# The masked products of the RWKV groups per head, over 64 rows, instead of over 128 rows with zeros

## The chip, the cores and the metric

One core of a Trainium2 chip runs the whole program. The metric is the device time of one execution in microseconds (us). TensorE is called PE in the profile (its weight loads PEld), VectorE DVE, ScalarE ACT, GpSimd POOL and SyncE SP.

## The reference

Two networks run one after the other on 512 positions of width 1024. The second has an RWKV mixer in its first layer; that is where the change lies. For each of 8 heads of width 64, and in both directions, the reference runs a scan over 768 positions (256 of context, 512 of the sequence):

```python
def _rwkv7_scan(S0, r, w, k, v, kk, a):
    def step(S, inp):
        r_t, w_t, k_t, v_t, kk_t, a_t = inp
        sa = jnp.einsum('bhvk,bhk->bhv', S, kk_t)
        S = (S * w_t[:, :, None, :] - sa[..., None] * (kk_t * a_t)[:, :, None, :]
             + v_t[..., None] * k_t[:, :, None, :])
        return S, jnp.einsum('bhvk,bhk->bhv', S, r_t)
    xs = tuple(jnp.swapaxes(t, 0, 1) for t in (r, w, k, v, kk, a))
    S, ys = lax.scan(step, S0, xs)
    return jnp.swapaxes(ys, 0, 1), S
```

Everything else of the reference (two blocks of the first network with attention and a convolution, the second network's differential attention, its second layer with two other scans, the MLPs) is computed before or after this stage and is not touched.

## The kernel before

The kernel computes the scan in chunks of 64 positions. Features lie on the partitions: two heads of 64 features fill the 128 rows, so 8 heads are 4 pairs. Each pair has 3 groups of 256 positions (4 chunks) and 2 directions, which makes 4 x 3 x 2 = 24 groups. `rwkv_group` (line 1537) prepares one group without the running state, `rwkv_chain` (line 1667) then carries the state through its 4 chunks.

A group first scales the features by powers of the decay: `AR` (lines 1553 to 1557) holds the scaled kk (index 0) and r (index 1) of each chunk, for each head e in columns of its own. Its tile is [128, 4 chunks, 2 kinds, 2 heads, 64], and the rows of head e are filled only in the columns of head e; the other half was set to zero once, at line 1359, and stays zero. `BK` (lines 1558 to 1560) holds the scaled k·a and k, [128, 4, 2, 64]. Then come the masked products (lines 1563 to 1571): for each chunk j one float32 matmul with BK of the chunk as weights (128 rows, 128 columns) and AR of the chunk as the moving operand (128 rows, 256 columns). Because of the zeros each column gets the sum over one head's 64 rows alone. Two chunks fill a PSUM bank of 512 columns; then DVE multiplies the bank by the causal mask into `Mh`, [128, 4, 2, 2, 64]. A group has 4 such matmuls and 2 such products. Each float32 matmul appears in the trace as two records.

After that ACT copies the part of Mh that belongs to kk to `AV`, one head at a time (line 1581), and a triangular system is solved in five levels: PE lines 1612, 1615 and 1628 (tile `lv`), ACT's copies at 1620 and 1625, DVE's predicated copies at 1602 and 1604, and at the end lines 1633 to 1649. BK and v are transposed at lines 1654 and 1661. In the chain, PE lines 1535, 1682, 1697, 1701 and 1704 (tile `z`) alternate with ACT's copies at 1685, 1693 and 1710 and DVE's update of the state at 1716.

The groups and chains are generators; `rwkv_drive` (line 1364) steps them by turns, up to three groups at once, and beside them the preparation of the next pair (`rwkv_prep`, with PE lines 1443, 1295, 1310) and the end of the last one (`rwkv_post`). The order of the instructions on an engine isn't written out: the framework's planner orders them when the program is built, by its own estimate of when each is ready. The four matmuls of a group stand together in the source, but in the program other lines' work is often put between them. PSUM banks of tag `mm`, three of them, are shared by the masked products, the transposes and the preparation; the levels have three (`lv`) and the chain two (`z`).

Of the kernel before, what the change touches and what calls it, by code (L numbers as in the profile page):

```python
# [15 lines left out]
ALU = mybir.AluOpType  # L16
# [4 lines left out]
P = 128  # L21
# [6 lines left out]
class Build:  # L28
# [1508 lines left out]
    def rwkv_group(self, d, g, n, r, k, v, kk, ka, L):  # L1537

        nc = self.nc
        TT = nc.vector.tensor_tensor  # L1540
# [12 lines left out]
        AR = self.ar[n % RWN[0]]  # L1553
        for e in range(2):
            rows = slice(64 * e, 64 * e + 64)
            TT(out=AR[rows, :, 0, e, :], in0=V4(kk)[rows], in1=G[rows, :, prev], op=ALU.mult)
            TT(out=AR[rows, :, 1, e, :], in0=V4(r)[rows], in1=G[rows, :, now], op=ALU.mult)
        BK = self.tl([P, 4, 2, 64], F32, "bk", "BK")
# [3 lines left out]

        Mh = self.tl([P, 4, 2, 2, 64], F32, "mh", "Mh")
        mk = self.masks[:, MSK[f"mh{d}"][0]:][:, :256]
        for j2 in range(2):
            ps = self.psum("mm")
            for j in (2 * j2, 2 * j2 + 1):
                nc.tensor.matmul(ps[:, (j % 2) * 256:(j % 2) * 256 + 256], BK[:, j].rearrange("p a t -> p (a t)"),  # L1568
                                 AR[:, j].rearrange("p a e t -> p (a e t)"), start=True, stop=True)
            TT(out=Mh[:, 2 * j2:2 * j2 + 2].rearrange("p j a e t -> p j (a e t)"),  # L1570
               in0=ps.rearrange("p (x t) -> p x t", x=2), in1=mk.unsqueeze(1).to_broadcast([P, 2, 256]), op=ALU.mult)
        yield


# [5 lines left out]
        for e in range(2):  # L1580
# [3 lines left out]
            in1=AV[:, :, 32 * d:32 * d + 32], op0=ALU.mult, op1=ALU.add)  # L1584
# [24 lines left out]
        for lev in range(1, 6):  # L1609
            w = 1 << lev  # L1610
            ps = self.psum("lv")
            nc.tensor.transpose(ps[:, 384:512], TV.rearrange("p j t -> p (j t)"), self.ident)
            W = NV if lev < 5 else AV[:, :, 32 * (1 - d):32 * (2 - d)]
            for j in range(4):
                nc.tensor.matmul(ps[32 * j:32 * j + 32, 0:64], W[:, j, :], half(D[:, j, :], d, w),  # L1615
                                 start=True, stop=True, skip_group_check=True)
# [6 lines left out]
            for j in range(4):  # L1623
                rows = slice(32 * j, 32 * j + 32)
# [11 lines left out]
           in1=jm.unsqueeze(1).to_broadcast([P, 2, 4, 32]), op=ALU.mult)  # L1636
# [3 lines left out]
        for b in range(4):  # L1640
            rows = slice(32 * b, 32 * b + 32)
            nc.scalar.copy(out=Tt[rows, :, rows], in_=blocks(F[rows]))
        yield
        for e in range(2):
            rows = slice(64 * e + 32 * d, 64 * e + 32 * d + 32)
            nc.tensor.matmul(ps[rows, 128:256], Bs[:, 32 * e:32 * e + 32], B[:, e].rearrange("p j c -> p (j c)"),
                             start=True, stop=True, skip_group_check=True)
# [4 lines left out]
        ps = self.psum("mm")  # L1652
# [6 lines left out]
        ps = self.psum("mm")  # L1659
# [862 lines left out]
```

## Time and profile before

| | us |
|---|---|
| median of 3 runs (3876.73 to 3882.26) | 3879.72 |
| the profiled execution | 3880.11 |
| its span in the profile | 3877.4 |

The profile is of one execution. A row of the groups view reads: line, engine, operation, tiles out<-in, shapes, count, then busy time in us and mean ns of one, then the idle time before them and what ended it. For a matmul `128*128 128x256` means weights of 128 rows and 128 columns and 256 columns of the moving operand. PEclk is the share of TensorE's full clock that was granted: 1.00 is 2.4 GHz, 0.50 is 1.2 GHz.

### The profile page before, as it was taken

Reading aid. Unit: us, or ns where it says so; the run is one execution under the profiler, and the core shown is the slowest. Engines: PE = TensorE matmul, PEld = TensorE weight load, DVE = VectorE, ACT = ScalarE, POOL = GpSimd, SP = SyncE. Lnnn points to the kernel's source line nnn. Section 1 sums busy time; section 2 is a strip of 40 time slices with the busy share of each in tenths; the row PEclk is TensorE's granted clock in tenths of the full one; section 3 lists DMA queues with packets and bytes.
Section 4 is the critical chain, followed back from the end, with each engine's and each line's share of the span. In section 5 each row is a group of like instructions: output and inputs, shape, how many; then the busy total and the mean of one; then the engine's idle time right before and its main releaser. Section 6 shows DMA issues by size and latency. Waiting matters only on the chain.

```text
span 3877.4 us, 54807 instructions
## 1 busy us (share of the span) xinstructions
PE 3686.8 (95%) x21434; PEld 2936.6 (76%) x21434; DVE 2388.8 (62%) x4168; ACT 1718.7 (44%) x3891; POOL 96.3 (2%) x205
## 2 busy tenths in 40 slices
PE   7789999999999999999998999999999999899998
PEld 5557888886678888788885666788888887688887
DVE  6578567675796565657646666554444575855444
ACT  4545343334653333335537788432222264634332
POOL 0000000000000000000001000000000000000000
PEclk8999999999999999999998999899999999889999
DMA  4332345442132355531110000211111212022232
GB/s 135 85 88 92 101 158 175 156 152 70 52 102 91 124 173 172 184 112 46 45 44 1 2 2 2 82 56 65 62 64 64 86 50 70 6 69 87 98 98 76
DMA packets 120322, 329.29 MB, mean 85 GB/s; under 512 B 12928, under 2 KB 38656, under 8 KB 120064
## 3 DMA queue, kind: packets, MB, share of 16 engines
q1 hardware_dynamic: 120064, 325.80, 26.1%
q8 instruction: 168, 2.75, 0.3%
q14 instruction: 90, 0.74, 0.1%
HBM read 311.46 MB, written 12.71 MB: 84 GB/s over the span
## 4 chain that ended last, share of the span: by engine, by line
PE 75%; issue 11%; ACT 6%; DVE 4%; POOL 1%; DMA 1%; SPq 1%; POOLq 0%; DVEq 0%; ACTq 0%
PE ps_g L232 20%; PE ps_g L230 20%; PE ps_g L231 20%; ACT B L1625 1%; PE ps_mm L1568 1%; DMA oh<-bkD 1%; PE ps_y L745 1%; POOL r L308 1%; PE ps_g L2169 1%; PE ps_z L1535 1%; PE ps_sc L735 1%; PE ps_y L1240 1%; DVE wlo L224 1%; PE ps_lv L1615 1%; PE ps_tr L339 1%
## 5 line engine op out<-in xcount | busy, mean ns | idle before, releaser
L230 PE MATMUL ps_g<-hi,whi 128*128 128x512 f32 (+1 forms) x4464 | 1666.6, 374 | 21.1 <-ACT whi L223 14.0
L232 PE MATMUL ps_g<-hi,wlo 128*128 128x512 f32 (+1 forms) x4464 | 1652.5, 371 | 16.7 <-DVE wlo L224 16.5
L231 PE MATMUL ps_g<-lo,whi 128*128 128x512 f32 (+1 forms) x3744 | 1400.5, 374 | 2.3 <-DVE lo L958 1.8
L223 ACT CAST whi<-raw 128x1024 fp32r<-128x1024 f32 (+3 forms) x497 | 481.6, 970 | 1246.0 <-PE ps_g L231 1067.1
L230 PEld LDWEIGHTS ps_g<-hi,whi 128*128 128x128 f32 x4464 | 845.9, 190 | 184.1 <-ACT whi L223 24.8
L232 PEld LDWEIGHTS ps_g<-hi,wlo 128*128 128x128 f32 x4464 | 845.1, 189 | 167.6 <-DVE wlo L224 24.5
L231 PEld LDWEIGHTS ps_g<-lo,whi 128*128 128x128 f32 x3744 | 709.8, 190 | 132.6 <-issue 7.3
L224 DVE TENSOR_TENSOR wlo<-raw,whi 128x1024 fp32r<-128x1024 f32 (+3 forms) x497 | 557.6, 1123 | 163.7 <-ACT whi L223 154.9
L231 PE MATMUL ps_g<-x,whi 128*128 128x512 f32 (+1 forms) x720 | 254.1, 353 | 0.0
L1134 DVE SCALAR_TENSOR_TENSOR x<-ps_g,mod,x 128x512 f32<-128x512 f32 (+1 forms) x192 | 127.1, 662 | 201.9 <-PE ps_g L232 201.8
L883 DVE SCALAR_TENSOR_TENSOR macc<-mraw,cs,macc 128x1024 f32<-128x1024 f32 x140 | 175.8, 1279 | 5.9 <-DMA mraw<-in_mod_w 5.6
L633 DVE SCALAR_TENSOR_TENSOR cv<-u,taps,cv 128x512 f32<-128x512 f32 x240 | 177.2, 745 | 1.2
L1113 DVE TENSOR_SCALAR r<-ps_g 128x512 f32<-128x512 f32 x96 | 57.7, 602 | 183.2 <-PE ps_g L232 180.4
L231 PEld LDWEIGHTS ps_g<-x,whi 128*128 128x128 f32 x720 | 138.4, 192 | 16.8 <-issue 1.6
L584 DVE TENSOR_TENSOR x<-ps_g,x 128x512 f32<-128x512 f32 x64 | 44.2, 690 | 138.6 <-PE ps_g L232 138.6
L1114 ACT ACTIVATE r<-r 128x512 f32<-128x512 f32 x96 | 53.3, 556 | 145.5 <-DVE r L1113 145.5
L468 DVE TENSOR_TENSOR o<-ps_g,R 128x512 f32<-128x512 f32 x76 | 52.2, 689 | 104.6 <-PE ps_g L232 99.8
L308 POOL TENSOR_TENSOR r<-v,mhalf 128x4 f32<-128x4 f32 (+2 forms) x30 | 38.2, 1273 | 2764.8 <-DVE v L327 2098.5
L577 DVE SCALAR_TENSOR_TENSOR r<-ps_g,R 128x512 f32<-128x512 f32 x64 | 44.0, 688 | 78.4 <-PE ps_g L232 75.2
L204 DVE TENSOR_TENSOR lo<-r,hi 128x512 fp32r<-128x512 f32 x96 | 57.6, 601 | 40.7 <-ACT hi L203 40.7
L1625 ACT COPY B<-ps_lv 32x64 f32<-32x64 f32 x384 | 77.7, 202 | 6.4
L291 ACT ACTIVATE sq<-x 128x512 f32<-128x512 f32 (+1 forms) x91 | 49.1, 543 | 69.7 <-DVE x L1134 33.9
(504 smaller groups left out, 4450.2 us busy)
## 6 DMA issues: line engine op xcount, KB each, us to landing
raw<-in_l_mlp_w SPq DMA_DIRECT2D x128, 512.0 KB
mraw<-in_mod_w SPq DMA_DIRECT2D x96, 512.0 KB
raw<-in_w_in SPq DMA_DIRECT2D x82, 512.0 KB
raw<-in_w_up SPq DMA_DIRECT2D x64, 512.0 KB
raw<-in_w_down SPq DMA_DIRECT2D x64, 512.0 KB
raw<-in_l_w_in SPq DMA_DIRECT2D x50, 512.0 KB
raw<-in_w_branch SPq DMA_DIRECT2D x48, 256.0 KB
bias<-biasD SPq DMA_DIRECT2D x32, 256.0 KB
```

What stands on the lines that cost most here:

```text
L204: nc.vector.tensor_tensor(out=lo, in0=src, in1=hi.bitcast(F32), op=ALU.subtract)
L223: nc.scalar.copy(out=hi, in_=raw)
L224: nc.vector.tensor_tensor(out=lo, in0=raw, in1=hi.bitcast(F32), op=ALU.subtract)
L230: t.matmul(ps, w[0], x[0], start=start, stop=False)
L231: t.matmul(ps, w[0], x[1], start=False, stop=False)
L232: t.matmul(ps, w[1], x[0], start=False, stop=stop)
L308: self.nc.gpsimd.tensor_tensor(out=r, in0=v, in1=self.mhalf[:, :v.shape[1]], op=ALU.pow)
L633: nc.vector.scalar_tensor_tensor(out=y, in0=u[:, j:j + T], scalar=taps[:, c * 31 + j:c * 31 + j + 1], in1=y, op0=ALU.mult, op1=ALU.add)
L883: nc.vector.scalar_tensor_tensor(out=acc[s], in0=rw, scalar=self.cs[:, k, s:s + 1], in1=acc[s], op0=ALU.mult, op1=ALU.add)
L1113: nc.vector.tensor_scalar(out=t, in0=ps[s][:, :n], scalar1=0.0, scalar2=None, op0=ALU.max)
L1134: nc.vector.scalar_tensor_tensor(out=xx[c], in0=ps[:, :n], scalar=md[:, s, 5, c:c + 1], in1=xx[c], op0=ALU.mult, op1=ALU.add)
L1625: nc.scalar.copy(out=B[rows, :, j, :], in_=blocks(ps[rows, 0:64]))
```

## The change

The two banks of a group are taken at once. For each chunk there are two matmuls, one per head: weights BK of 64 rows (the head's) and 128 columns, moving operand AR of the same 64 rows and the head's own 2 x 64 columns. Head 0 writes the first bank, head 1 the second, by turns. Each bank then holds four chunks of one head, and the mask product writes them to Mh with runs of 64. Mh has the same layout as before. The zeros in AR are no longer read by these matmuls; lines 1678 and 1704 still read them.

```diff
-        for j2 in range(2):
-            ps = self.psum("mm")
-            for j in (2 * j2, 2 * j2 + 1):
-                nc.tensor.matmul(ps[:, (j % 2) * 256:(j % 2) * 256 + 256], BK[:, j].rearrange("p a t -> p (a t)"),
-                                 AR[:, j].rearrange("p a e t -> p (a e t)"), start=True, stop=True)
-            TT(out=Mh[:, 2 * j2:2 * j2 + 2].rearrange("p j a e t -> p j (a e t)"),
-               in0=ps.rearrange("p (x t) -> p x t", x=2), in1=mk.unsqueeze(1).to_broadcast([P, 2, 256]), op=ALU.mult)
+
+        pe = [self.psum("mm") for _ in range(2)]
+        for j in range(4):
+            for e, ps in enumerate(pe):
+                rows = slice(64 * e, 64 * e + 64)
+                nc.tensor.matmul(ps[:, j * P:(j + 1) * P].rearrange("p (a t) -> p a t", a=2),
+                                 BK[rows, j].rearrange("p a t -> p (a t)"), AR[rows, j, :, e, :], start=True, stop=True)
+        for e, ps in enumerate(pe):
+            TT(out=Mh[:, :, :, e, :], in0=ps.rearrange("p (j a t) -> p j a t", j=4, a=2),
+               in1=mk.rearrange("p (a e t) -> p a e t", a=2, e=2)[:, :, e, :].unsqueeze(1).to_broadcast([P, 4, 2, 64]),
+               op=ALU.mult)
         yield
```

## Rows read from the trace of the kernel before

**Rows 1.** The page, part 1: busy us (share of the span) and instructions.
```profile
PE 3686.8 (95%) x21434; PEld 2936.6 (76%) x21434; DVE 2388.8 (62%) x4168; ACT 1718.7 (44%) x3891; POOL 96.3 (2%) x205
```
**Rows 2.** RWKV stage: stretch, length, busy (x) PE PEld DVE ACT POOL, PEclk, DMA, GB/s.
```profile
2053.00:2448.00 395.00, 357.94 (x4597) 237.00 (x4597) 264.94 (x740) 325.82 (x1316) 28.29 (x50) 0.92 0.02 6
```
**Rows 3.** Chain of waits by line, 2053 to 2448.
```profile
by line: ACT B L1625 10.7%; PE ps_mm L1568 10.3%; PE ps_z L1535 5.9%; PE ps_lv L1615 5.5%; PE ps_lv L1612 4.9%; ACT UV L1693 4.1%; PE ps_z L1697 3.9%; issue 3.9%; PE ps_lv L1628 3.7%; ACT tt L1620 3.5%; POOL hr L1304 3.3%; PE ps_mm L1443 3.
```
**Rows 4.** Groups by form, 2050 to 2420: the edited matmuls.
```profile
L1568 PE MATMUL ps_mm<-ar,BK 128*128 128x256 f32 x192 | 60.2, 440 | 10.6 <-DVE BK L1560 10.2 <-DVE Mh L1570 0.4
```
**Rows 5.** Timeline of PE, full clock (2344 to 2354), then half clock (2123 to 2128).
```profile
2344.58 0.70 PE L1568 MATMUL ps_mm<-ar,BK 128*128 128x256 f32 x2
...
2347.47 1.99 PE L1568 MATMUL ps_mm<-ar,BK 128*128 128x256 f32 x8
...
2350.78 2.86 PE L1568 MATMUL ps_mm<-ar,BK 128*128 128x256 f32 x12 [0.42 <-DVE Mh L1570]
...
2123.41 1.22 PE L1568 MATMUL ps_mm<-ar,BK 128*128 128x256 f32 x2
2124.56 0.64 PE L1646 MATMUL ps_lv<-B,bs 128*32 128x128 f32 x2
2125.12 2.36 PE L1568 MATMUL ps_mm<-ar,BK 128*128 128x256 f32 x6
```
**Rows 6.** Timeline of PE at line 794, another stage, full clock.
```profile
306.46 1.13 PE L794 MATMUL ps_sc<-o,q 64*128 64x256 f32 x8
...
263.26 0.72 PE L794 MATMUL ps_sc<-o,q 64*128 64x128 f32 x8
```
**Rows 7.** Timeline of PE at line 2169, another stage, half clock.
```profile
3396.64 1.06 PE L2169 MATMUL ps_g<-qd,kd 64*128 64x128 f32 x4
```
**Rows 8.** Groups by form, 2050 to 2420: mask products and like ones.
```profile
L1570 DVE TENSOR_TENSOR Mh<-ps_mm,msk 128x512 f32<-128x512 f32 x48 | 32.4, 688 | 17.4 <-PE ps_mm L1568 17.0
...
L1559 DVE TENSOR_TENSOR BK<-a,Gi 128x256 f32<-128x256 f32 x24 | 10.1, 419 | 1.7 <-PE ps_mm L1654 1.0 <-ACT Gi L1551 0.5
...
L1635 DVE TENSOR_TENSOR B<-ps_lv,msk 128x256 f32<-128x256 f32 x23 | 9.8, 424 | 9.6 <-ACT bs L1633 5.2 <-PE ps_lv L1646 4.3
```
**Rows 9.** Waits of ACT, 2050 to 2420: total us, times, longest.
```profile
ACT tt L1620 <- PE ps_lv L1615: 14.7, 25, 1.5
...
ACT av L1581 <- DVE Mh L1570: 3.9, 7, 0.9
ACT zs L1685 <- PE ps_z L1682: 3.6, 8, 0.8
ACT Tt L1649 <- PE ps_lv L1646: 3.3, 6, 1.3
```
**Rows 10.** Timeline of ACT, 2123 to 2135: instructions after a wait, in brackets.
```profile
2125.23 0.26 ACT L1649 COPY Tt<-ps_lv 32x128 f32<-32x128 f32 x1 [0.34 <-PE ps_lv L1646]
...
2127.90 0.21 ACT L1710 COPY y<-ps_z 128x64 f32<-128x64 f32 x1 [1.17 <-PE ps_z L1704]
...
2132.81 0.27 ACT L1620 COPY tt<-ps_lv 128x128 f32<-128x128 f32 x1 [0.81 <-PE ps_lv L1615]
...
2134.65 0.21 ACT L1685 COPY zs<-ps_z 128x64 f32<-128x64 f32 x1 [0.80 <-PE ps_z L1682]
```
**Rows 11.** Table of stretches: one around two groups' bursts.
```profile
2188.00:2195.00 7.00, 7.00 (x47) 4.66 (x45) 4.86 (x12) 6.65 (x25) 0.11 (x1) 1.00 0.00 1
```
**Rows 12.** Table of stretches: full clock, sparse, half clock, half clock.
```profile
2085.80:2119.90 34.10, 31.68 (x431) 20.39 (x430) 21.57 (x65) 30.89 (x122) 3.36 (x4) 1.00 0.01 2
2119.90:2123.40 3.50, 2.09 (x30) 1.43 (x30) 2.36 (x7) 3.29 (x15) 0.11 (x1) 0.99 0.03 7
2123.40:2126.80 3.40, 3.40 (x10) 2.09 (x9) 1.23 (x4) 2.89 (x12) 0.00 (x0) 0.51 0.00 0
...
2143.80:2154.10 10.30, 10.30 (x105) 6.63 (x105) 5.34 (x17) 6.83 (x30) 1.15 (x3) 0.50 0.01 2
```

## Prediction

> **What bounds the kernel now.** I read the page first: TensorE (PE) is busy for 95% of the span [rows 1], but that is an average over very different stages. The edit touches only lines that run in the RWKV stage, from 2053 to about 2448 us, so next comes the table of that stretch: of 395 us PE is busy 358, ScalarE (ACT) 326, VectorE (DVE) 265, at a mean granted clock of 0.92 [rows 2]. No engine is full. PE's figure counts the modelled tails of many short matmuls, and ACT at 82% is nearly as full. Then the chain of waits in that stretch: it passes through ACT's four small block copies (line 1625) for 10.7% and through the matmuls of line 1568, the ones that are edited, for 10.3%, that is 41 us [rows 3]. So these matmuls do lie on the path; the question is how much of it another engine takes over once they are shorter. The groups by form give their size: 192 records (two per float32 matmul, 96 matmuls) of 128x256, 60.2 us busy [rows 4].
>
> **What is removed, and what is put in its place.** A burst of line 1568 grows by 0.216 us with each record: two take 0.70, eight 1.99, twelve 2.86 ((1.99 - 0.70) / 6 = 0.215) [rows 5]. A group is four matmuls, eight records, so 1.99 us uncut at the full clock. Half of the products are with zeros: both heads stand in the 128 rows, and each column belongs to one of them.
>
> After the edit a group is eight matmuls, sixteen records, of 64 rows and 128 columns, head 0 and head 1 by turns into two banks. The trace already has this form elsewhere. At line 794 eight records of 64 rows and 256 columns, two heads by turns into two banks, take 1.13 us, as long as *four* full records do [rows 5, 6]: the two halves of the array run side by side. With 128 columns eight such records take 0.72 us [rows 6]. Going from 256 to 128 columns took 0.41 us off four pairs, so a pair's step fell by about 0.10, from 0.216 to 0.11. Sixteen records are then 0.72 + 4 x 0.11 = 1.16 us instead of 1.99: 0.83 us less per group, 24 x 0.83 = 20 us of PE time at the full clock. Taking the 60.2 us as they were, with cuts and low clock, in the same ratio gives 60.2 x (1 - 1.16 / 1.99) = 25 us. I carry 20 to 25 us of PE time freed.
>
> The bounds of that: the planner cuts a group's matmuls into pieces today (in the first row of the low-clock burst one matmul stands alone, and another line's work between it and the next three [rows 5]). If a cut falls inside a pair, the two halves run alone. An unpaired 64-row record of 128 columns at line 2169 takes (1.06 - 0.42) / 3 = 0.213 at the half clock [rows 7], so about 0.107 at the full one. With all pairs cut, 384 x 0.107 = 41 us stands against 192 x 0.216 = 41 us: nothing gained, nothing lost. So the freed time lies between 0 and 25 us, and I take the upper part, because line 794 is the same pattern.
>
> *DVE.* The mask product stays two instructions per group of 512 columns, now over all four chunks and one head, with runs of 64. They cost 0.688 us each [rows 8]. Runs of 64 in the output (line 1559, 0.419) and a PSUM input with a broadcast mask (line 1635, 0.424) cost the same for 256 columns [rows 8], so I take no change; even 0.05 us either way on 48 would be 2.4 us on an engine that is busy two thirds of the stage. What changes is the start: before, the first product ran beside the last two matmuls; now both banks are complete only at the end. From the first matmul to the end of the second product: 1.99 + 0.69 = 2.68 before, 1.16 + 2 x 0.69 = 2.54 after. So the group's own path is shorter by only 0.14 us, although PE is free 0.83 us sooner. ACT's two copies to AV (0.415 each) read one head each. If the first is released by the first product alone, another 0.4 us goes; the whole wait of AV for Mh is 3.9 us in 7 places [rows 9], which bounds it.
>
> So eviction, 0.69 per bank, is now longer than the 0.58 that PE needs to fill one. If it alone set each group's end, 24 x 0.14 = 3 us would be gained, 3877: that belongs to the second rival. The Trainium skill, "TensorEngine Tiling (Array Packing)", Performance Considerations, PSUM Bottleneck, says that tiling speeds up TensorE but not the evacuation of PSUM; by that rule the sum would end at this 3877, and the 0.688 us that doesn't shrink agrees with it.
>
> *PSUM.* Both banks are taken before the first matmul, out of three with tag mm. A bank was held for two matmuls and a product; now for the whole 1.16 us and one or two products: a few tenths longer for the second. Who would wait are lines 1443, 1654 and 1661 in the same tag, queued behind on PE. The wait of line 1568 for Mh today is 0.4 us in all [rows 4], so I put it at nothing; with one such 0.42 per pair of groups [rows 5] it would be 5 us.
>
> **How much of the freed PE time shows.** ACT has the least slack, so I ask where ACT waits for PE because of these bursts. Two pairs of groups are the ends. In 2123 to 2135 two groups' bursts go by, and ACT waits 1.17 us for line 1704 behind a burst, 0.81 for 1615, 0.80 for 1682, 0.34 for 1646: 3.1 us [rows 10]. In 2188 to 2195 two groups' bursts go by too, and ACT is busy 6.65 of 7.00 us, with no wait of note [rows 11]: there the freed time buys nothing at once. The mean of the two, 1.56 us, times 12 pairs is 19 us of ACT waiting near bursts; over the whole stage ACT's longest waits for PE (lines 1615, 1682, 1646) and for Mh add to 25.5 us [rows 9], so that isn't out of proportion. A burst that is shorter by 0.42 of itself (25 of 60.2) takes away about that share of the wait behind it: 19 x 0.42 = 8 us. The rest of the freed time becomes PE waiting for ACT (the copies of line 1625). So: 3880.1 - 8 = 3872 us. The profiled execution itself is 3880.1 (span 3877.4 and 2.7 around it), 0.4 above the median of the runs shown, so no correction.
>
> **The rivals.**
> *All of it shows* (0.10): the chain puts 41 us on line 1568; if ACT's order gives way, 41 x 0.42 = 17 us, and with the AV copies 20: 3860. For it: the chain. Against it: in 2188 to 2195 ACT has no room [rows 11].
> *Little or nothing shows* (0.17): ACT takes over at once, or DVE's eviction sets each group's end (0.14 us gained for each): 3880, from 3877 to 3884. For it: rows 11. Against it: the waits of rows 10.
> *The pairs don't run side by side, or the planner cuts them* (0.06): PE time as before, and for each further cut what a burst pays beyond its steps, 0.70 - 2 x 0.216 = 0.27 us [rows 5], at most 24 x 0.27 = 6 us: 3880 to 3886.
> *The clock falls: slower* (0.17). In this stage the granted clock drops to 1.2 GHz where PE has been sparse: in 2119.9 to 2123.4 PE is busy 2.09 of 3.50, and the next stretch is granted 0.51; it is back at 1.0 after that stretch, which was filled by eight records of line 1568 [rows 12]. The bursts are the densest work here, and the edit halves them. A low stretch costs: ACT is busy 0.66 of 2143.8 to 2154.1 and 0.91 of 2085.8 to 2119.9 [rows 12], so a quarter of the time is lost. The gain of 8 is gone when 32 us more are granted 1.2 GHz; beyond 64 the kernel is slower by 8: 3888. Some 63 us of the stage are low now (a mean of 0.92 over 395 us: 0.08 x 395 / 0.5 [rows 2]). Against it: the freed time pulls the other matmuls together. The Trainium skill, "TensorE: Matmul & The Clock Gate", Part 1, says that the throttled state is the default and activity releases it; the trace agrees where line 1568 precedes the rise, and the price above is from the rows.
>
> **How the numbers follow.** Forecast (0.50): part of the freed time shows, 3872, of itself 3860 to 3879, since the planner will also put other instructions in another order, which moves a few us either way. The range must leave out no more than 0.2: it reaches to 3858 for the full gain and to 3888 for the clock. What a measurement of this kernel can tell from no change is 0.2%, 7.8 us: faster is below 3872.0, slower above 3887.5. Faster: 0.10 from the full gain and 0.31 of the forecast's 0.50, as the copies to AV, up to 0.4 us a group, are not in the 8 us: 0.41. Slower: 0.14 of the clock, and 0.03 from cut pairs with lost order: 0.17. The rest, 0.42, can't be told from no change.
>
> **What would show it.** In the profile of after: line 1568 with 384 records, 64 rows, two starting together, bursts of 1.16 us per group and some 35 us busy instead of 60; the product at 0.69; ACT's share of the stage up by one or two points; the stage ending some 8 us sooner, everything after it shifted by as much. Wrong would be: eight pairs that take over 1.5 us, products over 0.75, more than 80 us at 1.2 GHz in the stage, or a stage of the same length in which line 1628's wait for ACT has grown by what line 1568 lost.

## The result and the profile after

The changed kernel takes 3929.35 us (median of 4 runs, 3917.39 to 3930.81), the kernel before 3880.99 beside it: a ratio of 1.0114, 95% interval 1.0098 to 1.013. It is slower by 1.1%, and above the range that was given. The profiled execution took 3917.39 us, span 3915.6, and is the fastest of the four. Ratios here and below leave out an execution that takes over 1.5% longer than the fastest of its kernel; only e4 has such executions, three of ten, and its median is that of all ten.

The table of stretches answers [rows 2]; its columns are the same. The first row is the part of the stage that [rows 2] shows, the second the whole stage, from the first memset of line 1549 to the last matmul of line 1522 (the bounds of all stage rows below):

```profile
2048.40:2488.00 439.60, 399.92 (x4790) 275.75 (x4791) 264.69 (x742) 327.24 (x1316) 27.64 (x51) 0.78 0.02 5
2047.40:2516.60 469.20, 425.77 (x5007) 293.69 (x5008) 276.21 (x772) 337.15 (x1350) 31.61 (x56) 0.79 0.04 14
```

And the whole stage in the kernel before:

```profile
2051.90:2476.30 424.40, 383.49 (x4815) 255.59 (x4816) 276.86 (x772) 335.68 (x1350) 32.37 (x56) 0.92 0.05 14
```

The stage is 44.8 us longer, the rest of the span 6.6 shorter (3915.6 - 469.2 against 3877.4 - 424.4), so all of the loss is here. ACT and DVE are busy as long as before (337 and 336 us, 276 and 277). What changed is the granted clock: 0.92 became 0.79. As it is 1.0 or 0.5, the time at 1.2 GHz is (1 - 0.92) x 424.4 / 0.5 = 68 us before and (1 - 0.79) x 469.2 / 0.5 = 197 us after. "us low" below is always this; as the view gives the clock to two decimals, each such figure is good to about 5 us.

The edited line and its product, groups by form, 2045 to 2465, for [rows 4] and [rows 8]:

```profile
L1570 PE MATMUL ps_mm<-ar,BK 64*128 64x128 f32 x384 | 66.5, 376 | 12.0 <-DVE BK L1560 9.9 <-DVE Mh L1573 1.2 <-DVE ar L1557 0.4
...
L1573 DVE TENSOR_TENSOR Mh<-ps_mm,msk 128x512 f32<-128x512 f32 x48 | 31.7, 684 | 30.8 <-PE ps_mm L1570 30.7
```

A line with half of the work in it is busy for longer than before, 66.5 us against 60.2. The product costs what it did, 0.684 us, but DVE waits 30.7 us for the matmuls, not 17. The chain of waits, 2048 to 2488, now has line 1570 ahead of ACT's copies of B, at 9.8% (before they stood at 10.7% and line 1568 at 10.3% [rows 3]):

```profile
by line: PE ps_mm L1570 9.8%; ACT B L1629 9.1%; PE ps_z L1535 6.4%; PE ps_lv L1619 5.3%; PE ps_lv L1616 4.9%; PE ps_mm L1443 4.1%; PE ps_z L1701 4.0%; ACT UV L1697 3.8%; PE ps_lv L1632 3.7%; issue 3.6%; PE ps_mm L1658 3.2%; PE ps_mm L1310 3
```

ACT's waits, 2045 to 2460 (total us, times, longest), are 1.6 to 2.3 times those of [rows 9]. Three of the four are for PE, at lines that the edit doesn't touch; the one of av is for the mask product:

```profile
ACT tt L1624 <- PE ps_lv L1619: 28.6, 32, 3.0
ACT zs L1689 <- PE ps_z L1686: 8.3, 10, 2.3
ACT av L1585 <- DVE Mh L1573: 7.9, 7, 3.1
...
ACT Tt L1653 <- PE ps_lv L1650: 5.4, 9, 1.2
```

So PE is late everywhere in the stage. Two theories can explain it. A: the granted clock fell, since the edited matmuls no longer work the array as they did, and everything on PE takes longer. B: the planner put the stage's instructions in another, worse order, and the clock only follows from the gaps in it.

### The profile page after: what moved, and what is told of

The parts are those of the page before. It is cut to its first block, busy times and chain, and to the rows that moved or that the text cites. A ratio compares the mean times of both kernels' runs of the same rounds, so it can differ in the third digit from the quotient of the medians.

```text
span 3915.6 us, 55182 instructions
## 1 busy us (share of the span) xinstructions
PE 3726.3 (95%) x21626; PEld 2972.3 (76%) x21626; DVE 2386.8 (61%) x4168; ACT 1719.6 (44%) x3891; POOL 97.0 (2%) x205
## 4 chain that ended last, share of the span: by engine, by line
PE 75%; issue 11%; ACT 6%; DVE 4%; POOL 1%; DMA 1%; SPq 1%; POOLq 0%; DVEq 0%; ACTq 0%
PE ps_g L230 19%; PE ps_g L232 19%; PE ps_g L231 19%; PE ps_mm L1570 1%; ACT B L1629 1%; PE ps_y L745 1%; POOL r L308 1%; DMA oh<-bkD 1%; PE ps_z L1535 1%; PE ps_sc L735 1%; PE ps_y L1240 1%; PE ps_lv L1619 1%; PE ps_mm L1443 1%; PE ps_lv L1616 1%; DVE wlo L224 1%
## 5 line engine op out<-in xcount | busy, mean ns | idle before, releaser
L232 PEld LDWEIGHTS ps_g<-hi,wlo 128*128 128x128 f32 x4464 | 845.1, 189 | 163.1 <-DVE wlo L224 19.8
L1606 DVE COPY_PREDICATED D<-msk,ps_lv 128x256 f32<-128x256 uint16 (+1 forms) x96 | 45.2, 471 | 57.4 <-PE ps_lv L1632 15.1
```

Of the source, the lines that this page charges most:

```text
L232: t.matmul(ps, w[1], x[0], start=False, stop=stop)
```

## The experiments

The stage rows and times of all kernels together; ratios are to the kernel before, timed on the same chip in the same job.

| kernel | median us | ratio (95%) | stage us | clock | us low |
|---|---|---|---|---|---|
| before | 3880.99 | | 424.4 | 0.92 | 68 |
| after | 3929.35 | 1.0114 (1.0098 to 1.013) | 469.2 | 0.79 | 197 |
| e1 all 128 rows | 3883.68 | 1.0004 (0.9991 to 1.0017) | 435.2 | 0.92 | 70 |
| e2 rows 0 to 63 for both heads | 3921.96 | 1.0107 (1.009 to 1.0125) | 477.9 | 0.77 | 220 |
| e9 rows 0 to 95 for both heads | 3922.96 | 1.0106 (1.008 to 1.0133) | 476.4 | 0.80 | 191 |
| e8 heads in turn | 3914.69 | 1.01 (1.0068 to 1.0133) | 465.9 | 0.80 | 186 |
| e6 128 and 64 rows by turns | 3946.31 | 1.0165 (1.0131 to 1.02) | 501.7 | 0.77 | 231 |
| e3 pairs twice | 3919.72 | 1.0094 (1.007 to 1.0117) | 455.0 | 0.90 | 91 |
| e5 full rows twice | 3901.45 | 1.0066 (1.0043 to 1.0089) | 454.5 | 0.95 | 45 |
| e4 after, 120 fillers | 3941.6 | 1.0108 (1.0067 to 1.0148) | 443.9 | 0.96 | 36 |
| e11 after, 96 late fillers | 3910.26 | 1.0076 (1.0054 to 1.0099) | 457.2 | 0.90 | 91 |
| e7 before, 120 fillers | 3897.46 | 1.0054 (1.0034 to 1.0073) | 453.5 | 0.95 | 45 |
| e10 before, 96 late fillers | 3892.83 | 1.0035 (1.0019 to 1.0051) | 439.3 | 0.97 | 26 |

The median of before was 3880.99 in after's job, 3881.44 in that of e1 to e4, 3878.90 in that of e5 to e8 and 3879.24 in that of e9 to e11. Stage, clock and us low are of the profiled execution. In e1, e6 and e9 every instruction of every engine stands in the order of the changed kernel; only the rows that line 1570 reads differ. In e2 the planner also placed some instructions otherwise, most of them PE's. e2 and e9 leave products out, as their expectations say, so they go on with other numbers; the changed kernel, e6 and e8 leave nothing out.

### e1: the changed form, but over all 128 rows

```diff
-                                 BK[rows, j].rearrange("p a t -> p (a t)"), AR[rows, j, :, e, :], start=True, stop=True)
+                                 BK[:, j].rearrange("p a t -> p (a t)"), AR[:, j, :, e, :], start=True, stop=True)
```

> The changed kernel, but each of the eight matmuls of a group reads all 128 rows of BK and AR again, zeros included; banks, products and the order of the instructions on every engine are exactly those of the changed kernel. A group's matmuls then take 16 x 0.11 = 1.8 us one after the other instead of 1.16 in pairs. Theory A (the clock: the halved bursts leave PE sparse, so more of the stage is granted 1.2 GHz): the stage's mean clock goes from 0.78 back to about 0.92 and the time to 3875 to 3895. Theory B (the planner's new order, with both banks complete only at the end, is slower by itself): the clock may be anything, the time stays at 3915 to 3935, if anything longer, since PE has more work.

It takes 3883.68 us, a ratio of 1.0004 that can't be told from the kernel before. The zeros are multiplied again, nothing runs side by side, and the time of the kernel before is back. Everything else of the change (two banks at once, their layout, the late first product, the planner's new order) is in this run and together costs nothing that can be measured in the whole. In the profiled execution e1's stage is 10.8 us longer than that of before with as much time low, and the rest of the span 4.2 us shorter (3884.0 - 435.2 against 3877.4 - 424.4); so the order does cost something in the stage, but not the loss. As the cause of the loss theory B falls.

Because the order is the same, equal pieces of work can be laid side by side. Rows of the table of stretches, one piece with 61 ACT instructions, in e1 and then in the changed kernel:

```profile
2260.90:2278.20 17.30, 16.67 (x249) 11.30 (x242) 11.66 (x39) 13.76 (x61) 1.25 (x4) 1.00 0.01 2
```

```profile
2274.00:2300.20 26.20, 26.17 (x242) 17.23 (x237) 12.17 (x39) 14.23 (x61) 1.24 (x4) 0.50 0.01 2
```

At 1.2 GHz throughout it takes 26.2 us, at the full clock 17.3: 8.9 of 26.2, or 0.34 of the low time, are lost. Another such piece, in the same view of the changed kernel and then of e1, takes 21.80 us against 15.30, 0.30:

```profile
2099.60:2121.40 21.80, 21.80 (x226) 13.85 (x228) 8.71 (x28) 14.14 (x61) 1.76 (x2) 0.50 0.01 2
```

```profile
2095.40:2110.70 15.30, 13.91 (x229) 9.12 (x229) 8.95 (x29) 13.64 (x62) 2.32 (x2) 1.00 0.01 3
```

Against e1 the changed kernel has 127 us more low and a stage that is 34 us longer.

### e2 and e9: half of the rows, and three quarters, with nothing side by side

e2 (e9 has `slice(0, 96)`):

```diff
-                rows = slice(64 * e, 64 * e + 64)
+                rows = slice(0, 64)
```

> The changed kernel, but both heads' matmuls use rows 0 to 63, so that no two of them can run side by side; the products of the second head are left out (they come out as zeros). The order on the engines is nearly that of the changed kernel (some 650 of 16400 lines of PE's listing differ). PE time per group about 16 x 0.11 = 1.8 us, as with full rows, but each with half of the array. Theory A, if the clock follows the time for which PE is busy: about as with full rows, 3875 to 3895, stage clock about 0.92. Theory A, if the clock follows how much of the array works: stage clock 0.78 or less and 3925 to 3945. Theory B: 3915 to 3935.

> The order of all instructions of the changed kernel. Both of a pair's matmuls read rows 0 to 95, so nothing runs side by side and all have one shape (the run with head 0 over 128 rows and head 1 over 64 turned out to pay for the change of shape between neighbours, which this one does not have). The second head's products are left out (rows 96 to 127 and the second head's lower rows are not summed as the reference has them); it is for the time alone. Theory 'the clock follows the share of the array's rows that work': between the 64-row run (3922, 217 us low in the stage) and the 128-row run (3884, 73 us low): about 3900. Theory 'only a full-height matmul keeps the clock': as the 64-row run, 3915 to 3930. Theory 'anything above one half is enough': 3878 to 3890.

Both go as the changed kernel does: 3921.96 and 3922.96 us. They can't run in pairs, and their matmuls take exactly as long as those of e1. The same burst, in the timelines of PE of e1 and of e9 (start, us, line, shapes, records), 1.60 us both times:

```profile
2311.16 1.60 PE L1570 MATMUL ps_mm<-ar,BK 128*128 128x128 f32 x12
```

```profile
2343.50 1.60 PE L1570 MATMUL ps_mm<-ar,BK 96*128 96x128 f32 x12
```

Where the clock is the same, so is everything else: with both traces cut at every 20th ACT instruction of the stage, 34 of the 67 pieces run at the full clock in both, and take 191.6 us in e1 and 191.7 in e9. Yet in the table of stretches the stage of e9 (below that of e1) is 41.2 us longer, at a clock of 0.80:

```profile
2049.80:2485.00 435.20, 388.78 (x5007) 273.09 (x5008) 274.83 (x772) 335.46 (x1350) 31.68 (x56) 0.92 0.05 15
```

```profile
2048.00:2524.40 476.40, 436.60 (x5007) 307.68 (x5008) 276.47 (x772) 336.76 (x1350) 31.64 (x56) 0.80 0.04 14
```

PE is busy for 0.92 of e9's stage and 0.89 of e1's, with the same count of instructions: the kernel whose PE looks busier is granted the lower clock (it looks busier in part because matmuls last longer at that clock). What differs between the two is 32 rows of the array that line 1570 reads or doesn't read. So it isn't gaps that brought the clock down, nor the pairing, but how many rows the edited matmuls work. The Trainium skill, "TensorE: Matmul & The Clock Gate", Part 1, says that the gate is set by how busy the PE has been recently; with e1 and e9 that agrees only if "busy" isn't read as the profile's busy column, which is the same for a matmul of 96 rows and one of 128 (1.60 us above).

It isn't in proportion to the rows either: e9 was expected near 3900 by the theory of shares, and 96 rows did as badly as 64. "Only a full-height matmul keeps the clock" came true of the three, for matmuls that run alone; for pairs see e3. By e9 the price is 41.2 us for 191 - 70 = 121 more us low, 0.34 each; by e2 42.7 for 150, 0.28.

### e8: both heads, but not by turns

```diff
-        for j in range(4):
-            for e, ps in enumerate(pe):
+        for e, ps in enumerate(pe):
+            for j in range(4):
```

> The changed kernel with the order of the two loops exchanged: head 0's four matmuls, then head 1's four, each over 64 rows. So both heads are computed, nothing runs side by side, the array is half used, and TensorE needs as long as before the change (16 x 0.108 = 1.7 us per group and more at the half clock). Theory 'pairing as such brings the clock down' (the array is busy for a shorter time): a clock as in the kernel before, 3880 to 3890. Theory 'half the rows at work bring it down, paired or not': 3915 to 3935, 170 to 220 us low in the stage, as the changed kernel. The first head's bank is complete half a burst sooner, worth at most 24 x 0.4 = 10 us, so 3910 would still agree with the second.

3914.69 us, 186 us low: the second theory; the time is just under its range and above the 3910 that it still allowed for. Bursts of eight records take 1.16 us here as they do in e1, so within them nothing overlaps; one of sixteen takes 1.49, so where one head's last and the other's first matmuls meet something still does. That half the rows bring the clock down, paired or not, is so shown by e2, in which nothing overlaps, and e8 agrees.

### e6: head 0 over 128 rows, head 1 over 64

```diff
-                rows = slice(64 * e, 64 * e + 64)
+                rows = slice(0, P) if e == 0 else slice(64, P)
```

> The order of all instructions of the changed kernel; head 0's matmul reads all 128 rows (its zeros included), head 1's its own 64 rows. So three quarters of the array's rows work on average, and nothing runs side by side. Theory 'the time follows the clock, and the clock the share of the array that works': between the full-row form (3884, 73 us low in the stage) and the changed kernel (3929, 196 us low): about 3900 with some 130 us low. Theory 'what matters is that TensorE is busy without gaps' (half rows do as well as full ones when they are not paired): as the full-row form, 3884; the run with unpaired half rows already speaks against it. In either case the price is about 0.33 us per us that is moved to the half clock.

This missed both expectations, 3946.31 us, the slowest of all. It was meant as a step between e1 and after, but neighbours of different heights pay for the change, as its timeline of PE has it for the burst shown above (the row names the shape of only one of the twelve records):

```profile
2357.81 2.57 PE L1570 MATMUL ps_mm<-ar,BK 64*128 64x128 f32 x12
```

2.57 us against 1.60, with the same matmuls around it and at the same clock: 0.08 us more per record. The Trainium skill, "TensorEngine Tiling (Array Packing)", Key Properties, says that changing the tiling mode drains the engine. The 0.08 us fit that; that draining is what takes them no run here shows. The run so mixes two effects and says nothing about the share of rows; e9 was made in its place.

### e3 and e5: each matmul twice, in pairs and over all rows

e3 (e5 reads `BK[:, j]` and `AR[:, j, :, e, :]` besides, as e1 does):

```diff
-        for j in range(4):
+        for j in (0, 0, 1, 1, 2, 2, 3, 3):
```

> The changed kernel, but each pair of matmuls is issued twice, the second time over the same result: 16 matmuls per group in pairs, so the form of the change with the PE time of before (2.0 us per group). Theory A: stage clock about 0.92, 3875 to 3895. Theory B: the new form stays, with more work: 3920 to 3940. The planner's order is new here, which may move either by some us.

> The same instructions in the same order as the run with each pair issued twice, but every matmul of line 1570 reads all 128 rows, zeros included, so that no two run side by side. TensorE then needs some 16 x 0.216 = 3.5 us per group at the full clock, where the paired form needs about 1.9. Both forms keep the array working, so the clock should be near 1.0 in both (low stretches under 100 us in the stage). The difference of the two times is what freed TensorE time is worth while the clock holds: 24 x 1.6 = 38 us of it. Theory 'TensorE time shows at 0.42, as the prediction had it': about 3920 + 16 = 3936. Theory 'freed TensorE time is hidden behind ScalarE': within 6 us of 3920. Theory 'the whole of it shows': 3958.

e3 has 91 us low, not 197, so the doubled pairs do hold most of the clock; but it takes 3919.72 us, where 3875 to 3895 was expected. e5 takes 3901.45, outside all three of its expectations, since those took the clock of both to be the same. The two have one order of instructions, and it is another than after's; that is why they are compared with each other and not with e1. Of e3's distance to e1, 12 us lie outside the stage (3916.3 - 455.0 against 3884.0 - 435.2), which the edit doesn't reach. By the clock of the whole span (0.962 against 0.968) some 28 us more are low there, which at a third each is 9 us of it; why they are low stays open. Inside the stage e3 is 19.8 us longer than e1: 21 us more are low, and line 1570 is busy for 93.6 us instead of 70.5, where the expectation had 24 x 2.0 = 48.

Between e3 and e5 the clock can be held. A piece of the same work at the full clock, rows of the table of stretches, e3 in pairs and then e5 over all rows:

```profile
2369.50:2390.50 21.00, 18.83 (x284) 14.41 (x284) 17.63 (x50) 15.59 (x62) 0.33 (x3) 1.00 0.01 2
```

```profile
2366.10:2389.50 23.40, 22.69 (x284) 18.68 (x283) 18.07 (x49) 15.69 (x62) 0.33 (x3) 1.00 0.01 1
```

Here the pairs save 2.4 us. Cut at every 20th ACT instruction of the stage, 49 of the 67 pieces run at the full clock in both: 294.2 us with pairs, 304.1 without. Line 1570 is busy for 51.9 and 71.7 us in them, so 19.8 us of PE time were freed and 9.9 us of it showed: 0.50. e3 loses them again: 46 us more low than e5, at a third each 15 us, and its stage is as long.

### e4, e11, e7 and e10: work put in to hold the clock

All four put a matmul of constants behind the level's four matmuls of line 1619 (before 1615). e4 in the changed kernel and e7 in the kernel before have it in all five levels, 120 in all:

```diff
                 nc.tensor.matmul(ps[32 * j:32 * j + 32, 0:64], W[:, j, :], half(D[:, j, :], d, w),
                                  start=True, stop=True, skip_group_check=True)
+            nc.tensor.matmul(ps[:, 256:384], self.ident, self.ones, start=True, stop=True, skip_group_check=True)
             if lev == 5:
                 break
```

e11 in the changed kernel and e10 in the kernel before have it in the first four levels, 96 in all:

```diff
             if lev == 5:
                 break
+            nc.tensor.matmul(ps[:, 256:384], self.ident, self.ones, start=True, stop=True, skip_group_check=True)
```

> The changed kernel with one more full matmul (128 rows, 128 columns, constants) per level of the triangular solve, 120 in all, into columns of the level's bank that nothing reads: 120 x 0.22 = 26 us more PE time, spread over the stage. Theory A: the stage clock rises over 0.9, and the time falls to 3870 to 3900 although work is added. Theory B: nothing gained, up to 26 us more: 3930 to 3955.

> The changed kernel with the same 96 added matmuls at the same place. Theory 'the changed kernel loses by the clock alone': the low stretches fall from 196 us to below 100, worth over 30 us, and the added 21 us cost 10 to 15: 3900 to 3915. If the fillers leave the clock where it was: 3935 to 3945. To beat the kernel before it would have to come below 3873.

> The kernel before with 120 matmuls added (128 rows, 128 columns, float32, of constants, into columns of the level's bank that nobody reads), one behind each of the first matmuls of a level. They take 120 x 0.22 = 26 us of TensorE time at the full clock. If the clock is worth 0.33 us per us at 1.2 GHz, the 71 us that are low in this kernel's stage are worth 24 us at most. Theory 'filling the gaps pays': 3865 to 3875. Theory 'the added work costs what it takes from the path, and the clock gives back no more than that': 3880 to 3895. With the changed kernel the same fillers left the time where it was or above it, so the second is the likelier.

> The kernel before with 96 added matmuls of constants (128 rows, 128 columns, float32, 0.22 us each at the full clock, 21 us in all), one behind the last of line 1615 of each level but the fifth, where ScalarE copies the level's results while the next matmuls of that level wait for it. In the kernel before TensorE is idle there for 12 us in all, so about half of the added time has cover. Theory 'what fills idle TensorE time is free, and gives back clock': 3865 to 3880. Theory 'the added time shows as it did behind line 1612 (26 us added, 19 more in the time, with 22 us less low)': 3890 to 3900.

The place of e7's matmuls isn't the one that its expectation and that of e10 name (the first matmuls of a level, line 1612): the edits differ in the fifth level alone. In all four the planner also moved other instructions. The clock rises in all four profiled executions; the table of stretches for the stage, of e11 and then of e10:

```profile
2053.30:2510.50 457.20, 416.23 (x5199) 289.85 (x5200) 275.42 (x772) 335.64 (x1350) 32.61 (x56) 0.90 0.04 14
```

```profile
2051.40:2490.70 439.30, 401.15 (x5007) 271.52 (x5008) 274.72 (x772) 336.04 (x1350) 33.22 (x56) 0.97 0.05 15
```

e11 is 19 us faster than the changed kernel (17 when each is taken against before in its own job) and so speaks for theory A from the other side: with nothing of the change undone, added work that nobody reads makes the kernel faster. 106 us less low are worth some 35 us; the rest, 16 us, is what 21 us of fillers cost. e4's executions lie from 3891 to 3956 us, at mean clocks from 0.974 to 0.949; its profiled one took 3900.2 with 36 us low, and the row in the table is that one's. So there the clock itself differs from one execution to the next of one program, and the time with it: from 3891.11 us (0.974) to 3945.00 (0.955) it is 54 us for 153 us more at 1.2 GHz, 0.35 each. For either theory of its expectation the run decides nothing, and why its clock varies stays open. In the kernel before, where only 68 us are low, the fillers cost more than the clock gives back: 3897.46 (2.5 us above the higher of e7's two ranges) and 3892.83. "Free" for e10 was wrong: its stage grew by 14.9 us though 42 us less are low. The filler stands between the level's matmuls and ACT's copy to tt, which waits for it, 24.0 us in 39 places (2045 to 2460), where it waited 14.7 us for line 1615 [rows 9]. No kernel of these beats the kernel before.

## Why the prediction was wrong, point by point

*The pairs run side by side: right where they stand together.* The burst of twelve in the changed kernel's timeline of PE, at the full clock, takes 0.94 us; by the prediction's own steps it is 0.72 + 2 x 0.11 = 0.94.

```profile
2331.07 0.34 PE L1535 MATMUL ps_z<-zs,Tt 128*64 128x64 f32 x4
2331.33 0.94 PE L1570 MATMUL ps_mm<-ar,BK 64*128 64x128 f32 x12
2332.75 0.32 PE L1632 MATMUL ps_lv<-B,tt 128*32 128x64 f32 x8 [0.47 <-ACT B L1629]
2332.99 0.49 PE L1570 MATMUL ps_mm<-ar,BK 64*128 64x128 f32 x2
2333.41 0.34 PE L1701 MATMUL ps_z<-UV,KBt 128*64 128x64 f32 x4
```

But the planner cut many of the bursts, and short pieces often gain nothing. In the timelines of PE the same four records take as long in the changed kernel as in e1, at the full clock in both:

```profile
2305.51 0.71 PE L1570 MATMUL ps_mm<-ar,BK 64*128 64x128 f32 x4
```

```profile
2282.61 0.71 PE L1570 MATMUL ps_mm<-ar,BK 128*128 128x128 f32 x4
```

Burst by burst, against an unpaired burst of as many records at the same clock (0.27 us and 0.11 for each record at the full one), the pairs freed some 9 us of PE time at the full clock; this is an estimate from the timelines. So the term of 20 to 25 us was more than twice what was freed: the 9 us lie within the bounds that the prediction gave, 0 to 25, but not in the upper part that it took.

In e1 line 1701 comes 2.23 us after the burst of twelve starts (2311.16 to 2313.39), here 2.08 (2331.33 to 2333.41). Of the 0.66 us that the pairs freed in it, 0.47 became PE's wait for ACT's copies of B. That is the mechanism the prediction named ("the rest of the freed time becomes PE waiting for ACT").

*Products without change: right*, 0.684 us against 0.688. *Banks at nothing: near enough*, line 1570 waits 1.2 us for Mh instead of 0.4, and e1, which takes them the same way, costs nothing in the whole.

*Some 35 us busy on the line: wrong*, 66.5. The steps hold at the full clock for pairs that stand together; about half of the records ran at the other one, and many bursts are pieces of two records, as the row at 2332.99 is.

*Part of the freed time shows, 0.42 of it, 8 us: the share about right, the 8 us too large.* e3 against e5 gives 0.50 with the clock held, which of some 9 us is 5 us. The 8 were read from waits of ACT of which 1.51 of 3.1 us end inside or right behind a stretch at 0.51 (2123.4 to 2126.8) [rows 10, 12], so they were in part the clock's; the other 1.61 us alone give 0.42 x 12 x 1.61 / 2 = 4 us. A second reading of what the pairs give agrees as far as one execution goes: the stage of the changed kernel is 7.2 us shorter than that of e9, in the same order and with about as much time low (197 and 191 us). Their medians (3929.35 and 3922.96, in two jobs) don't show it.

*The clock: the step that failed.* The forecast's sum, 3880.1 - 8 = 3872, leaves the time at 1.2 GHz as it was, and this term, put at nothing there, came to some +43 us. The fall of the clock stood among the rivals, at 0.17. It is what happened, and the sign that was named for it, more than 80 us at 1.2 GHz, came true with 197; but three things in it were wrong. Its price, a quarter of the low time, was too small: the pieces give 0.30 and 0.34, e9 0.34, e2 0.28, e4's executions 0.35. Its extent wasn't estimated at all: the text says that 32 us more low cancel the gain and 64 make it a loss, but not how many to expect; there were 129 more than before. So the end that it put into the range, 3888, was the bound "twice what cancels", not a bound of the mechanism. And the argument against it, that the freed time pulls the other matmuls together, looked at gaps. e9 has no freed time and no pairs, and its clock fell as far. The prediction had the right row in hand, the low stretch that eight records of line 1568 fill ahead of the rise [rows 12], and the right sentence, that these bursts are the densest work here; but it went by the time that PE is busy. That each edited matmul works half as many rows was in hand too; that rows count, no row of before shows, and it took e1, e2 and e9 to see it.

With the sizes measured: -5 for the freed time, +129 x 0.33 = +43 for the clock. That makes 38 us over the profiled 3880.1, and the profiled execution of the changed kernel is 37 above it. That it meets so closely is luck: the new order, which e1 has alone, is left out of the sum (e1's span is 6.6 us above that of before), and the low times are good to 5 us only. The median is 48 above that of before: in the three executions that weren't profiled the mean clock was 0.948 to 0.949 and not 0.953, and 0.0045 of 3925 us is 35 us more at 1.2 GHz, some 12 us.

## What to carry to other kernels

Where a stage sits between the two clocks, ask of each edit not only how much PE time it frees but which matmuls work the whole array there now; multiplying zeros over 128 rows can be what pays for the clock of everything around it. Price such an edit on the whole stage at both clocks (here about a third of each us that turns low), and let that bound set the range. To tell "the clock" from "the order", keep the order and change only the rows that are read: one such run settles it.

## What was not expected of the hardware

- The granted clock followed the rows that a matmul reads, at equal time: 70 us low with 128 rows and 191 with 96 in one order of instructions (e1, e9), 220 with 64 in nearly the same (e2). Pairs of 64 rows that were issued twice had 91 (e3, in another order). Between 96 and 64 there was little difference. How the chip weighs this no run here shows.
- Zeros do for it: e1's rows hold zeros in half of what the array multiplies.
- Matmuls of 128 and of 64 rows by turns cost 0.08 us more per record than either kind alone (e6, 2.57 against 1.60 us for twelve records).
- Added matmuls that nobody reads made the changed kernel faster, by 19 us (e11), and the kernel before slower, by 14 (e10).
- Time went with the clock without any edit too: executions of e4 took 54 us longer with 153 us more at 1.2 GHz.
